# A third staging buffer, earlier loads of a group's mixes, and down products woven between them, in a one-core hybrid encoder layer

## The chip, the core and the metric

The kernel runs on one core of a Trainium2 chip. The core has five engines, each with a queue of its own that it works through in order: TensorE (PE; its weight loads are listed apart as PEld), VectorE (DVE), ScalarE (ACT), GpSimd (POOL) and SyncE (SP), which here issues nearly all of the DMAs. An instruction that has to wait holds up everything behind it in its engine's queue. The metric is the time in microseconds (us) from start to end of one execution.

## The reference, cut to what matters

One encoder layer over 2048 prompt rows and 128 sample rows (8 sequences of 16), 17 tiles of 128 rows:

```
h = _rms(x, ln1_g)
p = h @ w_in
q, k, v, p_rw = jnp.split(p, (ATT_Q, ATT_Q + ATT_KV, ATT_COLS), axis=-1)
...
rw, wkv, shift_last = _rwkv(p_rw, shift_prev, wkv0, ...)
x = x + jnp.concatenate([att, rw], axis=-1) @ w_out
u = jax.nn.relu(_rms(x, ln2_g) @ w_up)
x = x + (u * u) @ w_down
```

`att` is attention over a window of 192 keys with a learned sink, 8 query heads on 2 key heads. `_rwkv` is a recurrence that runs from one tile to the next (a state of 64 x 64 for each of 8 heads), which the kernel does in chunks of 64 rows, with a small triangular solve for each chunk. D_MODEL is 1024, the hidden width 4096.

## The kernel before, in words

Every large product is done as three fp32r products (high part times high part, high times low, low times high), so a weight is held as a pair `w2` of a high and a low half, 1024 columns each. The first time that a weight is used, its raw fp32 copy is loaded into a staging tile `ws`; ACT casts the high half (line 128), POOL subtracts to get the low half (two instructions, line 131), and POOL's queue stores the pair to DRAM as `wp` (line 133). Every later use loads the pair straight from `wp` (line 120).

The work has two phases. In the first, four groups of tiles are projected (`project`, line 204, PE). In the second, `feed_forward`, five groups go through the output projection (`out_proj`, L1175), the norm, `up` (L1217, 32 weights) and `down` (L1239, 16 pairs of weights, each one product of 512 columns for a tile and a half of the output). The groups are tiles 0-2, 3-5, 6-8, 9-11, and 12-15 with the sample tile. The first of them (group 0) uses every weight for the first time.

The side streams run beside these main loops: attention (`att_stream`, one tile after another), the preparation of a tile's recurrence (`prep_stream`, `rw_prep` and `solve`) and the recurrence itself (`chain_stream`). `Weaver` is a planner that writes out the program's order: each yield of the main loop adds its assumed cost to a clock, and a side stream is stepped when its due time has come. A stream's step says how many units its result will need (`r[0]`) and what it costs (`r[1]`); its next step is due at `clock + r[0] * pace`. One pace holds for all streams: 0.75 in the first phase, 0.88 in the second. A scheduler then sorts each engine's queue further, from a model of when each instruction could start. So all orders are fixed when the program is built.

Between the phases `wv.finish(att)` steps the streams until attention has ended; only then are the pools of the second phase opened. At the start of a group its tiles' *mixes* (the rows of attention and recurrence side by side, `mr`, in DRAM) are loaded into `ws` (`load_mix`, L1102), split into a high and a low part (`ghh`, `ghl`; ACT L83 and DVE L84), and the half that is not yet transposed goes through PE (L1130). `ws` is one pool of two buffers, shared by the mixes and the raw weights. `Group.stages` gives four steps, one mix each and a flush that emits the last transposes; a step emits the transposes of the mix before it. After these four steps follow the six products of the old group's last `down`, and then the new group's output projection.

Of the kernel before, what the change touches and what calls it, by code (L numbers as in the profile page):

```python
# [1 line left out]

# [5 lines left out]
F32 = mybir.dt.float32  # L8
# [6 lines left out]
P = 128  # L15
D = 1024
# [17 lines left out]
def hymba_kernel(  # L34
# [52 lines left out]
    def pool(stack, name, **kw):  # L87
        kw.setdefault("reuse_waits", "tile")
        return stack.enter_context(tc.tile_pool(name=name, bufs=1, **kw))
# [27 lines left out]
    def weight_parts(key, w2, n, stage, src):  # L117

        if key in parts:
            sy.dma_start(out=w2.bitcast(F32), in_=parts[key])  # L120
            return
        ws = stage()
        if callable(src):
            src(ws)
        else:
            sy.dma_start(out=ws, in_=src)
        wh, wl = w2[:, 0:n], w2[:, n:2 * n]
        ac.copy(out=wh, in_=ws)  # L128
        for c0 in range(0, n, 512):
            c = slice(c0, min(c0 + 512, n))  # L130
            gp.tensor_tensor(out=wl[:, c], in0=ws[:, c], in1=wh[:, c].bitcast(F32), op=ALU.subtract)  # L131
        parts[key] = dram.tile([P, 2 * n], F32, name=f"wp{len(parts)}")
        gp.dma_start(out=parts[key], in_=w2.bitcast(F32))
# [768 lines left out]

    class Weaver:
        def __init__(self):
            self.clock, self.mains, self.pace = 0.0, [], 0.75

        def add(self, gen):
            m = [gen, self.clock, None]
            self.mains.append(m)
            return m  # L910

        def step(self):

            for m in self.mains:
                if m[1] > self.clock or (m[2] and not m[2]()):
                    continue
                m[2] = None
                try:
                    r = next(m[0])
                except StopIteration:  # L920
                    self.mains.remove(m)
                    return True
                if callable(r):
                    m[2] = r
                else:
                    self.clock += r[1]
                    m[1] = self.clock + r[0] * self.pace
                return True
            return False

# [80 lines left out]
    def att_stream(atp):  # L1011
        for t in range(NTP):
            yield lambda: bool(roped)
            yield from att_tile(t, atp, roped.pop(0))


# [3 lines left out]
    def prep_stream():  # L1020
        for j, t in enumerate(order):
            yield lambda: (t, 8) in projected
            if j and order[j - 1] == SMP:
                yield lambda: SMP in done
            loaded = rw_load(t)
            yield 6, 0
            g = rw_prep(t, rp, loaded, rwc["so"][j % 2])
            for r in g:
                if r != "tail":
                    yield r  # L1030
                    continue
                yield lambda: j == 0 or order[j - 1] in done
                try:
                    next(g)
                except StopIteration as e:
                    ready.append(e.value)
            yield 1, 1

    def chain_stream():
        for t in order:  # L1040
            yield lambda: bool(ready)
            pr = ready.pop(0)
            yield 3, 0
            yield from rw_sample(pr, rp) if t == SMP else rw_chain(pr, rp, STB)
            done.add(t)

    wv = Weaver()
# [7 lines left out]
    with ExitStack() as sst:  # L1055
        m = wv.add(att_sample(pool(sst, "satt")))
        wv.run(in_proj(first, (3, 4, 5)))
        wv.finish(m)
    ast = ExitStack()
    atp = pool(ast, "att")  # L1060
    att = wv.add(att_stream(atp))
    wv.add(rope_stream(atp))
    wv.run(in_proj(first, (6, 7, 8), group_of(1)))
    rw_constants()
    chain, prep = wv.add(chain_stream()), wv.add(prep_stream())
# [8 lines left out]
    cp = pool(ctx, "cp")  # L1074
# [4 lines left out]
    def load_w(key, src):  # L1079

        w2 = cp.tile([P, 2048], F32R, name="w2", bufs=3)
        weight_parts(key, w2, 1024, lambda: cp.tile([P, 1024], F32, name="ws", bufs=2), src)
        return w2[:, 0:1024], w2[:, 1024:2048]

    def load_wout(n):
# [12 lines left out]
    loaded = {}  # L1098

    def load_mix(t):  # L1100
        m = cp.tile([P, D], F32, name="ws", bufs=2)
        sy.dma_start(out=m, in_=mr[t])  # L1102
        return m

# [144 lines left out]
    members = [[0, 1, 2], [3, 4, 5], [6, 7, 8], [9, 10, 11], [12, 13, 14, 15, SMP]]  # L1249
# [13 lines left out]
    def steps(todo):  # L1263
        for c, fn in todo:
            g = fn()
            if c:
                yield c
            elif g:
                yield from g

    def feed_forward():
        def wait_for(tiles):
            while not done.issuperset(tiles):
                yield None

        def loads(g):
            return [(0, lambda t=t: g.load_y(t)) for t in g.tiles]

        yield from wait_for(members[0])
        cur, last = group(0), None  # L1280
        mixes, rest = cur.stages()
        yield from steps(loads(cur) + mixes + rest)
        for g in range(LAST + 1):
            todo, nxt = [], None
            for i in range(32):
                if i == 31 and 0 < g < LAST - 1 and done.issuperset(members[g + 1]):
                    for t in members[g + 1][0:2]:
                        loaded[t] = load_mix(t)
                yield from cur.up(i)
                if i == 0 and last:  # L1290
                    yield from last
                if g == LAST - 1 and nxt is None and len(done) == len(order):
                    nxt = group(g + 1)
                    mixes, rest = nxt.stages()
                    todo = loads(nxt) + mixes + rest
                if i >= 2 and i % 2 == 0:
                    yield from cur.down(i // 2 - 1)
                if todo:
                    k = -(-len(todo) // (32 - i))
                    yield from steps(todo[:k])  # L1300
                    todo = todo[k:]
            last = cur.down(15)
            if g < LAST and nxt is None:
                if g == LAST - 1:
                    yield from last
                    last = None
                yield from wait_for(members[g + 1])
                nxt = group(g + 1)
                mixes, rest = nxt.stages()
                yield from steps(mixes)  # L1310
                if last:
                    yield from last
                    last = None
                yield from steps(loads(nxt) + rest)
            cur = nxt
        yield from last

    wv.pace = 0.88
    wv.run(feed_forward())


# [103 lines left out]
```

## Time and profile before

| | us |
|---|---|
| median of 3 runs | 3117.43 |
| lowest and highest | 3111.29 and 3127.98 |
| the profiled execution, its own time | 3127.03 |
| its span, first to last instruction | 3125.2 |
| PE busy in the span | 2924.8 (94%) |
| DVE busy | 1797.7 (58%) |
| ACT busy | 910.8 (29%) |
| POOL busy | 737.3 (24%) |

The profiled execution is one of its own and lies 0.3% above the median of the three. PE is busy nearly all the time, so the table alone doesn't show where time could be lost. For that one reads stretches: how long PE was busy in each, and at which clock ("PEclk" is the share of full speed that was granted, 1.00 or 0.50 at any moment, and a mean in between over a stretch). In a row of waits, "PE x <- DMA y" says that PE's next instruction x started only when the DMA into y had landed.

### The profile page before, as it was taken

What the parts mean: (1) busy time and instruction counts of PE and PEld (TensorE: products, weight loads), DVE (VectorE), ACT (ScalarE), POOL (GpSimd) and SP (SyncE); (2) the same over time, 40 slices, a digit from 0 to 9 for tenths busy, and PEclk for the clock granted to TensorE, in tenths of its full rate; (3) what the DMA queues carried; (4) which work ended last, traced back from release to release, by engine and by line L of the source; (5) the groups of instructions that cost most, each with busy time, mean ns of one, the idle gap of its engine ahead of it and who ended that gap; (6) DMA issues with size and microseconds to landing.
All of it is one profiled execution on the core that took longest, in us unless ns stands there. A gap on an engine that the chain in (4) does not pass through costs nothing. (4 is left out here: it accounts for less than half of the span.)

```text
span 3125.2 us, 52326 instructions
## 1 busy us (share of the span) xinstructions
PE 2924.8 (94%) x20566; PEld 2569.7 (82%) x20566; DVE 1797.7 (58%) x3386; ACT 910.8 (29%) x2398; POOL 737.3 (24%) x713
## 2 busy tenths in 40 slices
PE   7888999998997989989999989999999999999999
PEld 7776877887886878778888878888888899999988
DVE  3346677564577586785666764666764424433444
ACT  5234335234333434332222223122232102111111
POOL 4553232231434566661110110111010000000000
PEclk8888998999998999999999998999999999999999
DMA  7665563664655778886666664666655756544443
GB/s 255 217 227 171 175 195 113 199 201 135 215 194 184 255 294 305 296 297 238 211 233 206 230 246 163 239 223 205 236 209 206 287 199 223 188 149 150 154 154 142
DMA packets 195089, 657.67 MB, mean 210 GB/s; under 512 B 33302, under 2 KB 92454, under 8 KB 148763
## 3 DMA queue, kind: packets, MB, share of 16 engines
q1 hardware_dynamic: 179290, 557.58, 53.0%
q0 software_dynamic: 15552, 96.74, 7.6%
q8 instruction: 163, 2.67, 0.3%
q14 instruction: 84, 0.68, 0.1%
HBM read 486.32 MB, written 154.68 MB: 205 GB/s over the span
## 5 line engine op out<-in xcount | busy, mean ns | idle before, releaser
L1217 PE MATMUL ffn<-ghh,w 128*128 128x384 f32 (+1 forms) x3072 | 779.7, 330 | 1.1 <-DVE ghl L138 0.6
L1239 PE MATMUL ffn<-w,sh 128*128 128x512 f32 x2176 | 706.8, 406 | 28.6 <-ACT sh L1223 13.0
L1217 PEld LDWEIGHTS ffn<-ghh,w 128*128 128x128 f32 x3072 | 546.6, 189 | 10.9 <-issue 4.1
L1241 DVE SCALAR_TENSOR_TENSOR y<-ffn,rs,y 128x512 f32<-128x512 f32 x544 | 401.1, 747 | 199.2 <-PE ffn L1239 197.6
L1239 PEld LDWEIGHTS ffn<-w,sh 128*128 128x128 f32 x2176 | 408.8, 193 | 122.2 <-ACT sh L1223 16.0
L1217 PE MATMUL ffn<-ghl,w 128*128 128x384 f32 (+1 forms) x1536 | 504.9, 329 | 0.0
L204 PE MATMUL acc<-w,hh 128*128 128x304 f32 (+1 forms) x2128 | 466.8, 311 | 37.5 <-DMA w<-wp 17.8
L1239 PE MATMUL ffn<-w,sl 128*128 128x512 f32 x1088 | 431.6, 401 | 1.7 <-DVE sl L1224 1.7
L204 PEld LDWEIGHTS acc<-w,hh 128*128 128x128 f32 x2128 | 355.0, 196 | 62.7 <-issue 19.9
L204 PE MATMUL acc<-w,hl 128*128 128x304 f32 (+1 forms) x1064 | 321.9, 305 | 0.3 <-DVE hl L138 0.3
L1222 DVE TENSOR_TENSOR tq<-tq 128x384 f32<-128x384 f32 (+1 forms) x192 | 113.6, 592 | 348.7 <-ACT tq L1221 347.8
L1217 PEld LDWEIGHTS ffn<-ghl,w 128*128 128x128 f32 x1536 | 290.2, 189 | 6.4 <-issue 1.9
L1221 ACT ACTIVATE tq<-ffn 128x384 f32<-128x384 f32 (+1 forms) x192 | 91.0, 474 | 687.8 <-PE ffn L1217 642.9
L1239 PEld LDWEIGHTS ffn<-w,sl 128*128 128x128 f32 x1088 | 209.1, 192 | 50.3 <-DVE sl L1224 3.3
L131 POOL TENSOR_TENSOR w<-ws,w 128x512 fp32r<-128x512 f32 (+1 forms) x166 | 216.6, 1324 | 133.4 <-ACT w L128 129.3
L204 PEld LDWEIGHTS acc<-w,hl 128*128 128x128 f32 x1064 | 208.8, 197 | 3.9 <-issue 3.0
L1223 ACT CAST sh<-tq 128x384 fp32r<-128x384 f32 (+1 forms) x192 | 95.1, 495 | 367.2 <-PE ffn L1239 204.2
L228 POOL TENSOR_TENSOR ev<-ev,eb 128x304 f32<-128x304 f32 x102 | 101.8, 1001 | 249.8 <-DVE eb L220 155.5
L1224 DVE TENSOR_TENSOR sl<-tq,sh 128x384 fp32r<-128x384 f32 (+1 forms) x192 | 118.9, 620 | 67.9 <-ACT sh L1223 67.2
L1175 PE MATMUL ffn<-w,ghh 128*128 128x256 f32 x768 | 152.2, 298 | 5.5 <-ACT w L128 2.8
L1175 PEld LDWEIGHTS ffn<-w,ghh 128*128 128x128 f32 x768 | 125.9, 200 | 10.6 <-ACT w L128 3.2
L209 ACT ACTIVATE ev<-acc,xr_rs 128x304 f32<-128x304 f32 (+1 forms) x153 | 76.0, 502 | 192.0 <-PE acc L204 111.1
(335 smaller groups left out, 4239.7 us busy)
## 6 DMA issues: line engine op xcount, KB each, us to landing
w<-wp SPq DMA_DIRECT2D x288, 1024.0 KB
wp<-w POOLq DMA_DIRECT2D x72, 1024.0 KB, 7.5
w<-wp SPq DMA_DIRECT2D x72, 608.0 KB
w<-wp SPq DMA_DIRECT2D x36, 512.0 KB
ws<-in_wup_dram SPq DMA_DIRECT2D x32, 512.0 KB
ws<-in_wdn_dram SPq DMA_DIRECT2D x32, 512.0 KB
pa<-ev SPq DMA_DIRECT2D x102, 152.0 KB
xs<-pa SPq DMA_DIRECT2D x68, 228.0 KB
```

The costliest lines, as they stand in the source:

```text
L131: gp.tensor_tensor(out=wl[:, c], in0=ws[:, c], in1=wh[:, c].bitcast(F32), op=ALU.subtract)
L204: pe.matmul(acc[:, 0:n], a[:, kk], b[:, c], start=(kk == 0 and m == 0), stop=(kk == 7 and m == 2))
L209: ac.activation(out=ev, in_=acc[:, 0:n], func=AF.Copy, scale=hT[t][2])
L228: gp.tensor_tensor(out=ev, in0=ev, in1=eb, op=ALU.subtract)
L1175: pe.matmul(pss[j // 2][:, o:o + 256], a[:, kk, self.col(t)], w[:, c], start=(kk == 0 and m == 0 and j % 2 == 0), stop=(kk == 7 and m == 2 ...
L1217: pe.matmul(ps, w[:, wc], a[:, kk, c], start=(kk == 0 and m == 0), stop=(kk == 7 and m == 2))
L1221: ac.activation(out=tq, in_=ps, func=AF.Relu)
L1222: ve.tensor_tensor(out=tq, in0=tq, in1=tq, op=ALU.mult)
L1223: ac.copy(out=sh[:, c], in_=tq)
L1224: ve.tensor_tensor(out=sl[:, c], in0=tq, in1=sh[:, c].bitcast(F32), op=ALU.subtract)
L1239: pe.matmul(ps, a[:, tc_], w[:, fc], start=(f == 0 and m == 0), stop=(f == 1 and m == 2))
L1241: ve.scalar_tensor_tensor(out=yt[:, c], in0=ps, scalar=self.rs2[t], in1=yt[:, c], op0=ALU.mult, op1=ALU.add)
```

## The change

Four things change.

1. The staging tiles `ws` get a third buffer, for mixes and raw weights alike.
2. While the last `up` of groups 1 and 2 is emitted, all three mixes of the next group are emitted as loads, not only the first two. (For the first group the loads stand in its own mix steps; for the last group in its own as well.)
3. The six products of the old group's last `down` no longer follow the mix steps in one block: after the second, the third and the fourth mix step two of them are emitted.
4. The pace is kept for each stream: attention's own stays 0.75 and becomes 0.5 from tile 12 on; the two recurrence streams have 0.75 in the first phase and 0.88 in the second, as before.

```diff
-            self.clock, self.mains, self.pace = 0.0, [], 0.75
-
-        def add(self, gen):
-            m = [gen, self.clock, None]
+            self.clock, self.mains = 0.0, []
+
+        def add(self, gen, pace=0.75):
+
+            m = [gen, self.clock, None, pace]
...
-                    m[1] = self.clock + r[0] * self.pace
+                    m[1] = self.clock + r[0] * m[3]
...
             yield lambda: bool(roped)
+            if t == 12:
+                att[3] = 0.5
             yield from att_tile(t, atp, roped.pop(0))
...
-        weight_parts(key, w2, 1024, lambda: cp.tile([P, 1024], F32, name="ws", bufs=2), src)
+        weight_parts(key, w2, 1024, lambda: cp.tile([P, 1024], F32, name="ws", bufs=3), src)
...
-        m = cp.tile([P, D], F32, name="ws", bufs=2)
+        m = cp.tile([P, D], F32, name="ws", bufs=3)
...
-                    for t in members[g + 1][0:2]:
+                    for t in members[g + 1]:
                         loaded[t] = load_mix(t)
...
-                yield from steps(mixes)
+                for k, step in enumerate(mixes):
+                    yield from steps([step])
+                    for c in islice(last or (), 0 if k < 1 else 2):
+                        yield c
...
-    wv.pace = 0.88
+    chain[3] = prep[3] = 0.88
```

The instructions are the same ones, in the same number on every engine; only their order and the buffers change. Line numbers of the changed kernel are higher by one up to line 900 or so and by four from line 1079 to 1306 (L1102 becomes L1106, L1130 becomes L1134, L1239 becomes L1243).

SP's queue at the start of group 0, before: `ws` from `mr` is a mix, `ws` from `in_wout` a raw weight, `y` the rows of x, `bk` and `mr15` belong to the recurrence and to attention's last tile.

```order
L1102 DMA ws_10744<-mr0_108 128x1024
L1102 DMA ws_10755<-mr1_109 128x1024
L635 DMA bk1_11821<-kk_10777 64x512
L636 DMA bk1_11821<-E2_10771 64x512
L343 DMA mr15_123<-qk_10278 128x512
L1138 DMA y_10738<-in_x_prompt_dram 128x1024
L1138 DMA y_10740<-in_x_prompt_dram 128x1024
L1138 DMA y_10742<-in_x_prompt_dram 128x1024
L1102 DMA ws_10792<-mr2_110 128x1024
L1090 DMA ws_10806<-in_wout_dram 64x2x256 x4
L816 DMA mr3_111<-yw_10525 128x512
```

The same place in the changed kernel:

```order
L1106 DMA ws_10722<-mr0_108 128x1024
L1106 DMA ws_10733<-mr1_109 128x1024
L1106 DMA ws_10766<-mr2_110 128x1024
L637 DMA bk0_11828<-E2_10814 64x512
L637 DMA bk1_11829<-E2_10814 64x512
L344 DMA mr15_123<-qk_10102 128x512
L1142 DMA y_10716<-in_x_prompt_dram 128x1024
L1142 DMA y_10718<-in_x_prompt_dram 128x1024
L1142 DMA y_10720<-in_x_prompt_dram 128x1024
L1094 DMA ws_10780<-in_wout_dram 64x2x256 x4
L127 DMA ws_10881<-in_wout_dram 128x1024
L1094 DMA ws_10945<-in_wout_dram 64x2x256 x4
```

The third mix now stands right behind the first two, and three raw weights, not one, stand ahead of the recurrence's `mr3`.

DVE's queue at the same moment, before: L84 subtracts for the mixes (from `ws` directly, and from the transposed half `ffn`), L653, L666 and L668 are the solve of one tile, L811 to L815 the end of another tile's recurrence.

```order
L618 TENSOR_TENSOR m_11131<-rk,cst 128x4x64
L653 STREAM_TRANSPOSE WS<-ma 32x512 x4
L811 TENSOR_TENSOR yw<-yw,gn_rs 128x512
L659 MEMSET WS 128x16
L84 TENSOR_TENSOR ghl<-ws,ghh 128x4x128
L84 TENSOR_TENSOR ghl<-ffn,ghh 128x4x128
L666 TENSOR_TENSOR tm<-WS 128x8
L84 TENSOR_TENSOR ghl<-ws,ghh 128x4x128
L84 TENSOR_TENSOR ghl<-ffn,ghh 128x4x128
L668 TENSOR_REDUCE WS<-tm 128x2x2
```

And in the changed kernel:

```order
L619 TENSOR_TENSOR m_11143<-rk,cst 128x4x64
L812 TENSOR_TENSOR yw<-yw,gn_rs 128x512
L85 TENSOR_TENSOR ghl<-ws,ghh 128x4x128 x3
L815 TENSOR_TENSOR yw<-yw,bv 128x512
L619 TENSOR_TENSOR ma<-rk,cst 128x4x64
L619 TENSOR_TENSOR m_11143<-rk,cst 128x4x64
L85 TENSOR_TENSOR ghl<-ffn,ghh 128x4x128 x3
L816 TENSOR_TENSOR yw<-yw,gs 128x512
L654 STREAM_TRANSPOSE WS<-ma 32x512 x4
L660 MEMSET WS 128x16
```

All six subtractions of the mixes moved ahead of the solve's four transposes; before, the first four stood behind them and the last two later still. PE's queue follows suit: from the first product of the output projection to the first product of that solve (`sv`, L704) stand 60 rows of L1175 before and 110 after.

PE's queue at the start of group 3 (tiles 9-11), before: `ffn<-cst,ws` transposes a mix, L704 belongs to a solve, L1239 is the old group's last `down`.

```order
L1217 MATMUL ffn<-ghh,w_22607 128x384
L1130 MATMUL ffn<-cst,ws 128x128 x8
L704 MATMUL sv<-so_2899,t_22536 64x64 x16
L704 MATMUL sv<-tm,t_22536 64x64 x16
L1130 MATMUL ffn<-cst,ws 128x128 x4
L1239 MATMUL ffn<-w_22691,sh 128x512 x2
```

The same place in the changed kernel, up to the second L704:

```order
L1221 MATMUL ffn<-ghh,w_22609 128x384
L1134 MATMUL ffn<-cst,ws 128x128 x4
L1243 MATMUL ffn<-w_22675,sh 128x512 x2
L1243 MATMUL ffn<-w_22675,sl 128x512
L1243 MATMUL ffn<-w_22675,sh 128x512 x2
L1243 MATMUL ffn<-w_22675,sl 128x512
L705 MATMUL sv<-so_2899,t_22536 64x64 x16
L1134 MATMUL ffn<-cst,ws 128x128 x4
L1243 MATMUL ffn<-w_22675,sh 128x512 x6
L1243 MATMUL ffn<-w_22675,sl 128x512
L1243 MATMUL ffn<-w_22675,sh 128x512 x2
L1243 MATMUL ffn<-w_22675,sl 128x512 x3
```

Six down products now stand between the first transposes and the solve, and twelve between the solve's first sixteen matmuls and its next (which follow the last row here); the third mix's transposes come eighteen products after the first's. The starts of groups 1 and 2 read alike.

## Rows read from the trace of the kernel before

**Rows 1.** The page: TensorE's busy time, share and instructions.

```profile
PE 2924.8 (94%) x20566; PEld 2569.7 (82%) x20566; DVE 1797.7 (58%) x3386; ACT 910.8 (29%) x2398; POOL 737.3 (24%) x713
```

**Rows 2.** Busy time of each engine by stretch; then granted clock, DMA share, GB/s.

```profile
944.00:970.00 26.00, 21.20 (x204) 16.61 (x204) 18.62 (x45) 15.79 (x56) 3.41 (x3) 0.87 0.28 77
970.00:1001.00 31.00, 15.28 (x105) 13.58 (x103) 30.10 (x49) 7.03 (x11) 17.11 (x14) 0.67 0.76 260
1051.00:1412.00 361.00, 335.20 (x2192) 284.73 (x2193) 267.84 (x395) 133.92 (x262) 230.42 (x206) 0.96 0.79 285
1412.00:1431.00 19.00, 13.03 (x114) 9.83 (x113) 10.56 (x17) 6.11 (x10) 6.14 (x6) 0.66 0.59 211
1826.00:1837.00 11.00, 7.08 (x35) 5.73 (x34) 5.44 (x10) 7.67 (x25) 1.64 (x1) 0.72 0.55 192
2244.00:2255.00 11.00, 7.42 (x58) 6.03 (x53) 7.51 (x16) 6.47 (x18) 0.73 (x1) 0.69 0.61 227
2436.00:2446.00 10.00, 6.48 (x24) 4.90 (x23) 4.43 (x7) 1.79 (x3) 0.00 (x0) 0.83 1.02 419
```

**Rows 3.** Waits: us in total, times, longest (PE: whole run; ACT: 985 to 1410).

```profile
PE ffn L1130 <- DMA ws<-mr: 14.8, 4, 8.4
...
PE ffn L1239 <- ACT w L128: 3.9, 2, 2.6
...
ACT w L128 <- DMA ws<-in_wup_dram: 45.6, 19, 5.0
```

**Rows 4.** Timeline of PE, start of group 0; idle time before in brackets.

```profile
979.73 1.11 PE L1130 MATMUL ffn<-cst,ws 128*128 128x128 f32 x4 [8.37 <-DMA ws<-mr]
983.63 0.80 PE L1175 MATMUL ffn<-w,ghh 128*128 128x256 f32 x2 [2.79 <-ACT w L128]
...
1000.04 1.02 PE L704 MATMUL sv<-so,ma 64*64 64x64 f32 x26 [1.94 <-DVE so L689]
```

**Rows 5.** Timeline of SP's queue, start of group 0.

```profile
960.96 0.91 SPq L1102 DMA_DIRECT2D ws<-mr  x2
...
975.75 0.33 SPq L1102 DMA_DIRECT2D ws<-mr  x1
977.49 2.67 SPq L1090 DMA_DIRECT2D ws<-in_wout_dram  x4
```

**Rows 6.** Timelines of DVE and of POOL, start of group 0.

```profile
970.15 4.20 DVE L653 STREAM_TRANSPOSE WS<-ma 32x512 f32<-32x512 f32 x4
...
975.01 0.67 DVE L84 TENSOR_TENSOR ghl<-ws,ghh 128x512 fp32r<-128x512 f32 x1
...
984.23 1.77 DVE L84 TENSOR_TENSOR ghl<-ws,ghh 128x512 fp32r<-128x512 f32 x1
...
983.66 3.48 POOL L131 TENSOR_TENSOR w<-ws,w 128x512 fp32r<-128x512 f32 x2 [1.99 <-ACT w L128]
...
990.58 2.56 POOL L131 TENSOR_TENSOR w<-ws,w 128x512 fp32r<-128x512 f32 x2 [2.51 <-ACT w L128]
```

**Rows 7.** Timeline of PE at the starts of groups 1, 2 and 3.

```profile
1415.04 1.15 PE L704 MATMUL sv<-so,ma 64*64 64x64 f32 x32 [2.29 <-DVE so L689]
1419.84 1.11 PE L1130 MATMUL ffn<-cst,ws 128*128 128x128 f32 x4 [3.66 <-DMA ws<-mr]
...
1830.10 1.29 PE L594 MATMUL rk<-cst,E 128*128 128x128 f32 x8 [2.48 <-ACT art L595]
1832.82 1.12 PE L1130 MATMUL ffn<-cst,ws 128*128 128x128 f32 x4 [1.44 <-DMA ws<-mr]
...
2246.43 1.25 PE L704 MATMUL sv<-tm,t 64*64 64x64 f32 x32 [2.25 <-ACT tm L717]
2249.01 1.11 PE L1130 MATMUL ffn<-cst,ws 128*128 128x128 f32 x4 [1.33 <-DMA ws<-mr]
```

**Rows 8.** The chain that ended last: start, us, what; undisturbed runs of two products.

```profile
2261.34 2.87 PE ffn L1175 x24
...
2335.03 4.32 PE ffn L1239 x18
```

More of the change, by code (lines that the diff above doesn't have):

```diff
@@ L1 @@
 from contextlib import ExitStack
+from itertools import islice
 import concourse.bass as bass
```

## The prediction

> **What bounds the kernel now.** The page comes first: TensorE is busy for 94% of the span and no other engine for more than 58% [rows 1]. So the kernel ends when PE's queue ends, and time can only come from two places: gaps in that queue, and stretches in which PE runs at the lower of its two clocks (1.2 instead of 2.4 GHz, a granted clock of 0.50 in the rows). The second view is the busy time by stretch [rows 2]. Its length minus PE's busy time is the gap; busy time times one minus the granted clock is roughly what the lower clock cost. The reader should see that the losses sit at the places that the change touches: the start of group 0 (970 to 1001) has 15.7 us of gaps in 31 us, at a mean clock of 0.67; the starts of groups 1, 2 and 3 (1412, 1826, 2244) have 6.0, 3.9 and 3.6 us of gaps, and clocks of 0.66, 0.72 and 0.69. Group 0's body (1051 to 1412) loses 25.8 us in gaps, spread thin. The third view, the waits, names who ends the gaps: PE's transposes of a mix waited four times for the load of that mix, 14.8 us in all, and PE waited twice for the cast of a raw weight, 3.9 us [rows 3]. Timelines then show each place.
>
> **The change, part by part.** Every engine executes the same instructions, so nothing is added or removed as work; each term is a wait that goes or comes.
>
> *Start of group 0.* SP issues the loads of mixes 0 and 1 at 960.96, but that of mix 2 only at 975.75, and the first raw weight at 977.49 [rows 5]: both had to wait until DVE had read a staging buffer. DVE's reading (L84, 0.67 us each) stood behind 4.20 us of solve transposes, from 970.15, and began at 975.01 [rows 6]. PE idled 8.37 us for mix 2 and 2.79 us for the first weight, and reached the solve's first product at 1000.04, after 1.94 us more of waiting for DVE [rows 4]. In the changed order mix 2 is loaded with the others, the six L84 come ahead of the 4.20 us, so three buffers come free early and three raw weights follow at once. But DVE was busy for 30.10 of the 31 us [rows 2], and its work only changes order, so the solve will not be ready much before 1000. What is gained is what PE has done by then: 110 rows of L1175 instead of 60. One such product takes 0.12 us (2.87 us for 24 [rows 8]), so 50 of them are 6 us. **Term: -6.** Bounds: 0, if the solve is late by as much as PE is early, and -10, about two thirds of the 15.7 us of gaps.
>
> One rule speaks against this term. The row shows an L84 of 1.77 us, against 0.67 us undisturbed, beside a pair of POOL subtractions of 3.48 us, against 2.56 us [rows 6]: two engines that slowed each other. The Trainium skill, page "SBUF — State Buffer", section "SBUF: two separate sides", says that VectorE with two SBUF inputs and GpSimd share a port pair as an exclusive lock, so one waits for the other. The rows agree, with 1.1 and 0.9 us for one meeting. The L84 now come before any POOL subtraction, but these come forward into the solve's own two-input work; if three of them met it, the term would be -3 instead of -6 and the sum -22 instead of -25. I keep -6, since POOL's work keeps its amount.
>
> *Starts of groups 1 to 3.* The gaps are six waits: three for a mix's load, 3.66, 1.44 and 1.33 us, and three for the recurrence, 2.29, 2.48 and 2.25 us [rows 7]; they sum to 13.4 us, as the stretches' gaps do. The lower clock adds 13.03 x 0.34 + 7.08 x 0.28 + 7.42 x 0.31 = 8.7 us [rows 2]. Every third mix now has a buffer of its own, and at groups 2 and 3 its load stands far earlier in SP's queue; at group 1 it is covered by the down products instead. So the 6.4 us of mix waits go. The recurrence's waits get cover: six down products between the first transposes and the solve, twelve and four transposes between the two solve steps at group 3. A down product takes 0.24 us (4.32 us for 18 [rows 8]), so that is 1.4 us and 3.4 us, against waits of 2.3 to 2.5 us; I take 5 of the 7.0 us. Of the lower clock I take 5 of 8.7 us, since PE's gaps mostly vanish. **Term: -16.** Bounds: -6, the mix waits alone, and -22, everything. What covered the splitting of the new mixes were the same down products; now the third mix has only six of them behind it (1.4 us), but the output projection begins with the half that needs no transposing, so I charge nothing for that; without this cover it would be one ACT and one DVE step, about 1.3 us by the L84 row, three times.
>
> *Raw weights in group 0.* ACT waited 45.6 us for raw up weights, 19 times [rows 3]. SP could load one only when POOL had read an old one. Most of this is hidden, since PE has products to do meanwhile; what reached PE is the 3.9 us of waits for the cast [rows 3]. **Term: -4**, bounds 0 and -6 (with a share of lower clock as at the groups' starts, 8.7 on 13.4).
>
> *Last group.* Between 2436 and 2446 PE lost 3.5 us of gaps and 6.48 x 0.17 = 1.1 us of clock [rows 2]. But the DMA engines were full there (share 1.02, 419 GB/s [rows 2]): a third buffer moves one mix ahead and moves no fewer bytes. **Term: -1**, bounds 0 and -5.
>
> *Attention's last tiles.* From 944 to 970 PE has only side streams to do: gaps of 4.8 us, 2.8 us of clock [rows 2]. In the new order 116 rows, not 150, stand between the last projection and the first mix. **Term: -2**, bounds -6 and, if attention's DVE steps now delay the recurrence's, +4.
>
> *Given back.* PE's stalls gave DVE time to catch up; without them DVE is late next, at the casts and solves in group 0, where it is busy for 268 of 361 us [rows 2]. **Term: +4**, bounds 0 and +12, half of the 25.8 us of gaps there.
>
> The sum is -6 - 16 - 4 - 1 - 2 + 4 = -25 us. The profiled execution took 3127.0 us, so it would take 3102; it lies 9.6 us above the median of the three runs shown, 3117.4, and on that footing the forecast is 3092 us. All bounds at their best give -49 (3068), all at their worst +10 (3127).
>
> **The rivals.** *A: the waits change their name.* PE's gaps at the groups' starts go, but come back as waits for DVE a few us later, since the recurrence has the same work to do per tile. For it: three of the six waits of [rows 7] are the recurrence's, and DVE was full at the start of group 0. Against it: in the body of group 0 DVE had 93 of 361 us free. Then only the mix waits of groups 1 to 3 are kept, with a little of the start: -8, 3109 us.
>
> *B: it does not do what it says.* The loads are earlier in SP's queue, but the DMA engines deliver them no earlier. For it: a DMA share of 0.76 to 1.02 in [rows 2]. Against it: the mix of 975.75 waited for a buffer, not for the engines. -3, 3114 us.
>
> *C: slower, through ACT's queue.* With raw weights there earlier, the cast L128 waits no longer for its input but for a free pair `w2` (three buffers, as before), which PE frees. In ACT's queue the cast then holds up the relu and cast behind it (L1221, L1223), on which PE's next products wait. The price is that of one cast wait, up to 2.6 us [rows 3]. Group 0 has 64 such weights; from the tenth such wait on (25 / 2.6) the gain is gone, and one weight in four makes 16 x 2.6 = 42 us: 3134 us. For it: those 19 waits of ACT must find a next reason. Against it: ahead of each L1221 ACT's queue holds as many L128 in both kernels, give or take one.
>
> **How the numbers follow.** Chances: the forecast 0.64, A 0.20, B 0.09, C 0.07. About 0.5% (15.6 us) is what a measurement of this kernel can tell from no change. Nearly all of the forecast's range (3068 to 3101) is faster by more than that, A and B are within it, C is slower: faster 0.63, same 0.30, slower 0.07. The range from 3068 to 3119 takes in the forecast, A and B; it leaves out C and the far ends.
>
> **What would show it.** In the profile after: no PE wait for `ws` from `mr` longer than a microsecond at groups 0 to 3; three mix loads side by side on SP near 960 and the first L1175 some 4 us after the mixes, with the first L704 still about 30 us after 970; clocks above 0.9 at the starts of groups 1 to 3; ACT's waits for raw weights well below 45.6 us with no waits of L128 for PE in their place. Wrong it would be if PE's waits for DVE and ACT results (L704, L1239) grew by more than 10 us in sum, if gaps remain where they were at the groups' starts, or if the end of attention came later than 970.

## The result, and the profile after

The changed kernel takes 3078.93 us (median of 4 runs, 3074.63 to 3083.32) against 3117.40 us of before in the same series: a ratio of 0.9874, 95% interval 0.9850 to 0.9898. That is 38.5 us less, where 25 were forecast. The profiled execution took 3074.63 us (span 3072.8), the one of before 3127.03. Of the 52.4 us between these two, 13.9 are scatter: the one of before lay 9.6 us above its median, that of after 4.3 us below.

The page, TensorE's line: busy share and count as in [rows 1], with less busy time because more of it runs at the full clock (granted clock 0.965 in the mean of the span, 0.957 before).

```profile
PE 2896.5 (94%) x20566; PEld 2554.5 (83%) x20566; DVE 1807.6 (59%) x3386; ACT 908.8 (30%) x2398; POOL 736.4 (24%) x713
```

Busy time by stretch, columns as in [rows 2]: attention's tail after the last projection, the start of group 0 up to its first `up`, and the starts of groups 1, 2 and 3.

```profile
937.00:959.90 22.90, 19.26 (x199) 14.64 (x198) 19.76 (x40) 16.23 (x51) 10.26 (x7) 0.93 0.49 144
959.90:1033.80 73.90, 55.38 (x484) 51.07 (x483) 46.01 (x88) 24.66 (x48) 38.41 (x37) 0.84 0.84 283
...
1391.00:1411.50 20.50, 16.96 (x103) 12.26 (x101) 19.18 (x30) 6.08 (x11) 5.51 (x5) 0.83 0.77 266
1800.50:1814.50 14.00, 13.46 (x86) 11.01 (x85) 10.99 (x19) 8.50 (x28) 4.13 (x3) 1.00 0.69 252
2198.00:2212.00 14.00, 14.00 (x136) 11.29 (x135) 11.76 (x22) 8.46 (x22) 1.29 (x1) 1.00 0.72 257
```

The starts of groups 2 and 3 have hardly a gap (0.54 us and none) and nothing of the lower clock any more. Group 1's start still has 3.5 us of gaps, and there DVE was busy for 19.18 of 20.5 us.

PE's waits over the whole run (total, times, longest). The four waits for a mix at groups 0 to 3 [rows 3] are gone. New are two waits at group 0's output projection, 7.6 and 6.9 us.

```profile
PE ffn L1179 <- DVE y L1184: 8.3, 2, 6.9
...
PE ffn L1179 <- DVE tm L667: 7.6, 1, 7.6
PE ffn L1243 <- DVE y L1245: 6.9, 8, 2.4
PE ffn L1243 <- ACT sh L1227: 5.7, 6, 2.5
...
PE sv L705 <- DVE so L690: 4.3, 3, 2.3
```

The timeline of PE at the start of group 0, which answers to [rows 4]: the transposes of all three mixes run at once, and then PE waits 7.57 us, and later 6.93 us for one of DVE's additions. The solve's first product (L705) follows at 996.63.

```profile
959.89 1.53 PE L1134 MATMUL ffn<-cst,ws 128*128 128x128 f32 x12
...
971.35 0.80 PE L1179 MATMUL ffn<-w,ghh 128*128 128x256 f32 x2 [7.57 <-DVE tm L667]
...
990.09 0.80 PE L1179 MATMUL ffn<-w,ghh 128*128 128x256 f32 x2 [6.93 <-DVE y L1184]
...
996.63 0.33 PE L705 MATMUL sv<-so,ma 64*64 64x64 f32 x2 [0.54 <-DVE so L690]
```

SP's queue at the same place, which answers to [rows 5]: three mix loads side by side, but the first raw weight only at 962.11, when the first mix had left its staging buffer.

```profile
949.94 1.39 SPq L1106 DMA_DIRECT2D ws<-mr  x3
...
962.11 2.66 SPq L1094 DMA_DIRECT2D ws<-in_wout_dram  x4
```

ACT cast that weight at 970.25, and PE began when the cast ended:

```profile
970.25 1.04 ACT L129 CAST w<-ws 128x1024 fp32r<-128x1024 f32 x1 [2.73 <-DMA ws<-in_wout_dram]
```

So the wait put down to DVE's `tm` is one for the first weight; the kernel e7 below, with the same order there, has 6.9 us at this place under the name of the cast.

ACT's waits from 972 to 1390. The 45.6 us for raw `up` weights [rows 3] are gone, and the cast (L129) now waits for a pair `w2` that PE frees.

```profile
ACT w L129 <- PE ffn L1179: 27.1, 5, 10.6
...
ACT w L129 <- PE ffn L1243: 8.9, 10, 2.7
```

### The profile page after: what moved, and what is told of

Its sections match the earlier page's. It is cut to its first block, busy times and chain, and to the rows that moved or that the text cites. A ratio compares the mean times of both kernels' runs of the same rounds, so it can differ in the third digit from the quotient of the medians.

```text
span 3072.8 us, 52320 instructions
## 1 busy us (share of the span) xinstructions
PE 2896.5 (94%) x20566; PEld 2554.5 (83%) x20566; DVE 1807.6 (59%) x3386; ACT 908.8 (30%) x2398; POOL 736.4 (24%) x713
## 5 line engine op out<-in xcount | busy, mean ns | idle before, releaser
L1243 PE MATMUL ffn<-w,sh 128*128 128x512 f32 x2176 | 695.4, 402 | 21.0 <-DVE y L1245 6.9
L205 PE MATMUL acc<-w,hh 128*128 128x304 f32 (+1 forms) x2128 | 466.0, 311 | 34.9 <-DMA w<-wp 13.9
L1243 PEld LDWEIGHTS ffn<-w,sh 128*128 128x128 f32 x2176 | 403.8, 190 | 111.9 <-DVE y L1245 10.3
L1243 PE MATMUL ffn<-w,sl 128*128 128x512 f32 x1088 | 426.8, 397 | 1.9 <-DVE sl L1228 1.9
L1226 DVE TENSOR_TENSOR tq<-tq 128x384 f32<-128x384 f32 (+1 forms) x192 | 121.1, 631 | 342.6 <-ACT tq L1225 341.6
L1243 PEld LDWEIGHTS ffn<-w,sl 128*128 128x128 f32 x1088 | 206.3, 190 | 49.8 <-DVE sl L1228 3.9
L1228 DVE TENSOR_TENSOR sl<-tq,sh 128x384 fp32r<-128x384 f32 (+1 forms) x192 | 112.1, 584 | 62.7 <-ACT sh L1227 61.7
```

What stands on the lines that cost most here:

```text
L205: pe.matmul(acc[:, 0:n], a[:, kk], b[:, c], start=(kk == 0 and m == 0), stop=(kk == 7 and m == 2))
L1226: ve.tensor_tensor(out=tq, in0=tq, in1=tq, op=ALU.mult)
L1228: ve.tensor_tensor(out=sl[:, c], in0=tq, in1=sh[:, c].bitcast(F32), op=ALU.subtract)
L1243: pe.matmul(ps, a[:, tc_], w[:, fc], start=(f == 0 and m == 0), stop=(f == 1 and m == 2))
```

## The experiments

Eleven kernels were run. They are compared in stretches that begin at the last projection (the last row of L204), for a reason that the last section gives. **Tail** is from there to the first mix transposes; **start 0** from these to group 0's first `up`; **body 0** from there to its last `up`; **starts 1-3** the sum of the three stretches from a group's last `up` to the next group's first output projection product; **A** is from the last projection to the first product of group 1's output projection, **B** from there to the last group's. What follows B is 627 us in every kernel. All in us, one profiled execution each; the ratio is to the kernel before in the same series, whose median lies between 3113.7 and 3117.8 us.

| kernel | median | ratio (95%) | tail | start 0 | body 0 | starts 1-3 | A | B |
|---|---|---|---|---|---|---|---|---|
| before | 3117.4 | 1 | 30.8 | 80.8 | 360.4 | 65.1 | 497.6 | 1060.8 |
| after | 3078.9 | 0.9874 (0.9850-0.9898) | 22.9 | 73.9 | 357.2 | 47.6 | 474.4 | 1034.2 |
| e1 buffer | 3091.8 | 0.9923 (0.9908-0.9938) | 30.5 | 72.2 | 352.5 | 51.4 | 478.5 | 1037.5 |
| e2 weave | 3103.3 | 0.9957 (0.9942-0.9972) | 30.8 | 79.4 | 359.1 | 58.2 | 500.4 | 1030.6 |
| e3 pace | 3105.2 | 0.9965 (0.9947-0.9982) | 22.0 | 83.5 | 353.5 | 63.0 | 484.1 | 1051.8 |
| e4 no weave | 3085.4 | 0.9904 (0.9885-0.9922) | 22.6 | 74.9 | 350.8 | 51.7 | 471.9 | 1035.7 |
| e5 no pace | 3089.3 | 0.9926 (0.9907-0.9946) | 30.5 | 74.6 | 353.9 | 48.0 | 479.9 | 1036.9 |
| e6 third mix | 3091.7 | 0.9933 (0.9911-0.9954) | 22.4 | 78.1 | 362.3 | 50.5 | 486.1 | 1042.5 |
| e7 two early | 3080.1 | 0.9879 (0.9856-0.9903) | 22.4 | 73.6 | 357.6 | 47.6 | 473.9 | 1036.2 |
| e8 first weight | 3079.8 | 0.9896 (0.9871-0.9920) | 22.5 | 73.5 | 353.5 | 52.3 | 474.6 | 1034.9 |
| e10 pace 0.3 | 3082.4 | 0.9903 (0.9888-0.9918) | 27.0 | 67.6 | 355.0 | 48.2 | 470.7 | 1037.9 |
| e11 early group 1 | 3075.7 | 0.9875 (0.9853-0.9896) | 23.6 | 74.6 | 352.9 | 53.6 | 477.4 | 1030.7 |
| e12 POOL subtracts | 3074.3 | 0.9867 (0.9843-0.9891) | 22.4 | 80.7 | 345.8 | 47.8 | 469.6 | 1036.6 |

The stretches don't hold the same work in every kernel. Counted where each begins, start 0 has 517 matmuls before, 483 in after and 455 to 561 elsewhere, because steps of the recurrence move between it and body 0. So start 0 alone doesn't show what an edit is worth. Start 0 and body 0 together have 2698 to 2705 matmuls in every kernel and can be compared: 441.2, 438.5, 436.9 and 440.4 us where raw weights have two buffers (before, e2, e3, e6), and 422.6 to 431.2 us in the nine kernels where they have three. (The profiled executions of before, e2 and e6 lie 5 to 10 us above their medians, that of e3 2 us below.) Busy time of before in these two stretches, then of e6; the count of matmuls here takes in those that overlap an edge:

```profile
970.30:1051.10 80.80, 60.46 (x518) 54.16 (x516) 49.19 (x100) 29.47 (x61) 44.88 (x40) 0.79 0.78 272
1051.10:1411.50 360.40, 334.70 (x2188) 284.27 (x2189) 267.30 (x393) 133.84 (x261) 230.32 (x206) 0.96 0.79 286
```

```profile
965.50:1043.50 78.00, 58.10 (x528) 53.30 (x528) 48.23 (x103) 28.64 (x60) 42.53 (x40) 0.85 0.80 281
1043.50:1405.80 362.30, 338.96 (x2172) 287.23 (x2171) 271.49 (x383) 134.13 (x260) 229.40 (x206) 0.96 0.78 284
```

**e1: the third buffer alone,** on the kernel before.

```diff
-        ... name="ws", bufs=2)
+        ... name="ws", bufs=3)
```

> The third buffer alone, on the kernel before. Theory (each gain belongs to the part that the prediction gave it to): start of group 0 -6, raw weights -4, last group -1, and at the starts of groups 1 to 3 the waits for mixes, 6.4 us, with their share of the lower clock (8.7 us on 13.4 of gaps), so -10: together -21, about 3096 us; the recurrence's waits stay at the groups' starts. Rival 1 (the waits change their name: without the weaving, the transposes that no longer wait for a mix stand behind the recurrence's waits, which grow by as much): only start, raw weights and last group are left, -11, about 3106 us. Rival 2 (what was gained is an accident of the order, not of the buffer): any time, with group 0's transposes still waiting.

26.1 us faster in its series (3117.84 to 3091.77). The theory's size holds, rival 1 falls: the starts of groups 1 to 3 lose 13.7 us without any weaving. Start 0 is 8.6 us shorter, but by work that left it (62 matmuls, 10.2 us of PE's busy time) and not by its gaps, which are 22.0 us instead of 20.3. What the theory did not say is where the start of group 0 loses time now. In the timeline of PE the wait for mix 2 is gone, and one for the first weight stands in its place:

```profile
992.60 0.79 PE L1175 MATMUL ffn<-w,ghh 128*128 128x256 f32 x2 [11.18 <-ACT w L128]
```

**e2: the weaving alone,** on the kernel before.

```diff
-                yield from steps(mixes)
+                for k, step in enumerate(mixes):
+                    yield from steps([step])
+                    for c in islice(last or (), 0 if k < 1 else 2):
+                        yield c
```

> The weaving alone, on the kernel before: two buffers, two mixes loaded early. Theory: six or twelve down products cover the third mix's load as well as the recurrence's waits, so most of the 13.4 us of gaps at the starts of groups 1 to 3 goes, with its clock: -16, about 3101 us, while the start of group 0 keeps its 8.4 us wait for mix 2 and its 2.8 us wait for the first weight. Rival 1 (the third buffer is what takes the mix waits away, and the third mix's load still waits for a buffer): only the recurrence's part, about -8, 3109 us. Rival 2 (the waits change their name): -3 or less, 3114 us.

14.5 us faster: the theory's size, but not its place. Starts 1 to 3 give 6.9 us in all, while B is 30.2 us shorter; 10.2 us of that lie in group 2's output projection and norm (64.1 us to 53.9). At groups 2 and 3 weaving by itself empties the starts as well as the buffer does (13.2 and 14.0 us, of 20.2 and 19.3). At group 1 it makes the start longer, 31.0 us instead of 25.6, with 32 more matmuls of the solve in it. SP's queue shows one reason: with two buffers, the third of that group's mixes is loaded only behind a raw weight of the last `down`, and the next raw weight (1430.22) behind that mix:

```profile
1422.53 0.33 SPq L127 DMA_DIRECT2D ws<-in_wdn_dram  x1
1429.79 0.32 SPq L1103 DMA_DIRECT2D ws<-mr  x1
1430.22 0.37 SPq L127 DMA_DIRECT2D ws<-in_wdn_dram  x1
```

PE then waits for that weight's cast, with the third mix's transposes behind it:

```profile
1438.65 0.80 PE L1240 MATMUL ffn<-w,sh 128*128 128x512 f32 x1 [3.91 <-ACT w L129]
```

**e3: the pace alone,** on the kernel before, with a pace for each stream as in the change.

```diff
...
+            if t == 12:
+                att[3] = 0.5
...
```

> Attention's pace alone, on the kernel before. Theory: it shortens the end of attention, -2 as predicted or -7 as the trace of the changed kernel reads (from attention's 898 row to its last store 71.8 us before, 64.7 after), and nothing behind it: 3110 to 3115 us, with first transposes some 7 us earlier and group 2's output projection as long as before (64 us). Rival (the pace shifts the recurrence against the groups, so that other waits go, the 9 us of group 2's output projection among them): -15 or more, 3102 us or below.

12.6 us faster, more than the theory, less than the rival. The tail is 8.8 us shorter, and body 0 6.9 us; start 0 gives 2.6 us back: 12 more matmuls stand in it, and PE still waits for mix 2 there, 9.01 us. Group 2's output projection and norm took 59.0 us, neither the 64.1 of before nor the 54.7 of after.

**e4: the change without the weaving.**

> The changed kernel without the weaving: the old group's six last down products stand in one block behind the mix steps again. Theory: mixes have their buffer and are loaded early, so only the cover of the recurrence's waits is lost, 5 to 7 us of gaps with their clock: +8, about 3087 us, with the starts of groups 1 to 3 each some 3 us longer. Rival 1 (the weaving is what empties the starts, and the early loads do nothing by themselves): +17, about 3096 us. Rival 2 (the weaving does nothing that the buffer does not): the changed kernel's 3079 us.

3085.35 us: the theory (+8; by the medians 6.4 came, by the ratios 9.4). Starts 1 to 3 are 4.1 us longer, 3.3 of them at group 1; rival 1 falls. Rival 2 is told apart by these starts alone, since the intervals of the two ratios overlap. Once there is a third buffer, weaving pays at group 1 and little elsewhere: B is 1.5 us longer.

**e5: the change without the pace.**

> The changed kernel with attention's pace left at 0.75 throughout; buffer, early loads and weaving stay. Theory (the pace shortens the stretch from the last projection to the first mix transposes, 30.8 us in the three kernels without it and 22 to 22.9 us in the three with it, and does nothing behind it): that stretch is 31 us again and the time +8, about 3087 us. Rival 1 (most of what the pace alone brought, 12.6 us, came from later stages, through a shifted recurrence): +12 or more, 3091 us or above, with longer stretches at groups 1 and 2. Rival 2 (the next work is late anyway, so the shorter tail is given back at the start of group 0): +2 or less, 3081 us.

3089.25 us, and the tail is 30.5 us again. The place is the theory's, the size lies between it and rival 1 (+10 by the medians, +16 by the ratios, +8.2 by the traces from the last projection on). How the pace pays is in the busy time by stretch. The first phase up to the last projection, tail and start 0 of e5:

```profile
0.00:940.40 940.40, 836.26 (x6401) 728.66 (x6402) 530.56 (x1130) 368.39 (x1089) 344.36 (x376) 0.93 0.58 191
940.40:970.90 30.50, 25.70 (x262) 19.54 (x261) 22.83 (x50) 17.70 (x60) 6.84 (x7) 0.89 0.33 100
970.90:1045.50 74.60, 51.16 (x456) 48.69 (x455) 46.13 (x89) 25.07 (x48) 42.53 (x38) 0.82 0.85 286
```

The first phase of after:

```profile
0.00:937.00 937.00, 834.18 (x6451) 727.46 (x6452) 538.16 (x1140) 369.15 (x1098) 339.77 (x376) 0.94 0.59 192
```

With the pace 62 matmuls of attention and the recurrence leave the tail (258 to 196), and 50 more run before the last projection (6401 to 6451). In e3 the same 62 leave and the same 50 come. So most of the work that left the tail moved forward, into the first phase. What it costs there can't be told: the first phase ends anywhere from 937.0 to 950.1 us in these kernels. Start 0 has 28 matmuls more than in e5 (455 to 483, 51.16 to 55.38 us of busy time) at nearly the same length, 74.6 and 73.9 us: its gaps take them up (23.4 us in e5, 18.5 in after).

**e6: the third buffer for a third mix only;** raw weights stay at two.

```diff
-        ... lambda: cp.tile([P, 1024], F32, name="ws", bufs=3), src)
+        ... lambda: cp.tile([P, 1024], F32, name="ws", bufs=2), src)
...
-        m = cp.tile([P, D], F32, name="ws", bufs=3)
+        own = t < 12 and t % 3 == 2
+        m = cp.tile([P, D], F32, name="mx" if own else "ws", bufs=1 if own else 2)
```

> The changed kernel with the third buffer given to mixes alone: the third mix of groups 0 to 3 has a staging tile of its own, and raw weights rotate through two buffers as before. Theory (raw weights are worth the predicted 4 us and more: without the third buffer for them group 0's body is some 7 us longer, by the 360.4 us of before against 352.5 with the buffer alone): ACT's waits for raw up weights are back at some 45 us, and the time is +4 to +8, 3083 to 3087 us. Rival (those waits of ACT are hidden behind PE's own work, and the third buffer pays by the mixes alone): the waits come back but the time stays at 3079 us.

3091.68 us, +12.8 by the medians and +18 by the ratios (0.0059 of 3117): beyond the theory's 8, and the rival falls. ACT's waits for raw weights are back, as its waits from 960 to 1430 show:

```profile
ACT w L129 <- DMA ws<-in_wup_dram: 39.3, 14, 5.7
ACT w L129 <- DMA ws<-in_wdn_dram: 33.4, 15, 5.9
...
ACT w L129 <- DMA ws<-in_wout_dram: 28.3, 4, 14.3
```

A is 486.1 us, no shorter than e3's 484.1, which has two buffers for everything, and start 0 and body 0 together, 440.4 us, are as long as without any third buffer: up to group 1 the third buffer pays by the raw weights, not by the mixes. By which waits of PE it pays isn't shown; those for the relu's cast (L1223 before) are 13.0 us before and 5.7 in after, but 13.1 in e1. The mixes' buffer shows at starts 1 to 3, which are 12.4 us shorter than e3's and 7.7 shorter than e2's, which has the weaving.

**e7: only two mixes loaded early.**

```diff
-                    for t in members[g + 1]:
+                    for t in members[g + 1][0:2]:
```

> The changed kernel with only two of a group's three mixes loaded early, as before; the third is loaded in its own mix step. DVE's, ACT's and POOL's queues are the same as the changed kernel's; on SP the third load stands a few rows later, at groups 2 and 3 alone. Theory (buffer and weaving empty these starts, not the earlier load): the starts of groups 2 and 3 stay at 13.6 us each and the time at 3079 us, within 3. Rival (the third load's place on SP is what takes away the waits of 1.4 and 1.3 us for it): +3 to +5, 3083 us, with those two waits back.

3080.06 us, starts of 13.7 and 13.5 us, no wait for a mix at groups 2 and 3: the theory. The earlier third load does nothing that shows beside the buffer and the weaving.

**e8: the first raw weight loaded ahead.**

```diff
...
+        first = cur.pl.tile([P, D], F32, name="y", bufs=cur.nt)
+        load_wout(0)(first)
+        ahead["out", 0, 0] = first
```

> The changed kernel, with the first raw weight of group 0's output projection loaded ahead of the mixes, into a tile that one row of x takes over later. Theory (at the start of group 0 PE now waits 7.6 us for this weight, whose load stands on SP until a mix has left its staging buffer; the same place where the kernel with the buffer alone waited 11.2 us for the cast): that wait goes to below 1 us, the first product of the output projection comes some 7 us earlier, and since the second weight can't come earlier by as much, 4 us of it remain, one weight's products (36 of 0.12 us): 3075 us. Rival 1 (DVE is what paces this start, and its solve is no earlier): PE waits as long a little later, 3079 us. Rival 2: the second weight comes as much earlier too, and 7 us remain, 3072 us.

3079.82 us: rival 1's time, but not its mechanism. The first product comes 6.2 us after the first transposes instead of 11.5 (a wait of 2.35 us is left for the cast, then 2.27 for POOL's half), but from there to the first `up` it takes 67.3 us instead of 62.5, so that start 0 is 73.5 us, as in after. It holds 46 matmuls more, though (483 to 529), and its gaps are 13.1 us instead of 18.5: what filled the time is moved work, not a later wait. Start 0 and body 0 are 427.0 us (431.1 in after), but group 1's start is 25.1 instead of 20.4, and A is the same. The load itself moved only from 2.2 us after the first transposes to 0.7 us before them.

**e10: pace 0.3.** The 0.5 of the change becomes 0.3.

> The changed kernel with attention's pace 0.3 instead of 0.5 from tile 12 on. Theory (attention's end is bound by its own chain from step to step once its steps are emitted early enough; 0.5 has most of it): from the last projection to the first mix transposes 20 to 23 us, time within 3 us of 3079. Rival 1 (steps emitted earlier still go on paying as from 0.75 to 0.5): another -5, 3074 us. Rival 2 (attention's steps then delay the recurrence on DVE, which group 0 needs later): +4 or more, 3083 us.

3082.40 us: the time is the theory's; its tail is not (27.0 us, at a granted clock of 0.72), and start 0 is shorter by as much and more (67.6). The two together are 94.6 us against 96.8 of after. They hold 44 matmuls fewer; 28 more run before the last projection and 35 more in body 0, so work changed its stretch again.

**e11: two mixes of group 1 loaded early.**

```diff
-                if i == 31 and 0 < g < LAST - 1 and ...
-                    for t in members[g + 1]:
+                if i == 31 and g < LAST - 1 and ...
+                    for t in members[g + 1][0:3 if g else 2]:
```

> The changed kernel, with the first two mixes of group 1 also loaded while the last up of the group before is emitted; in the changed kernel they wait on SP behind raw weights, and group 1's start is 20.4 us long where those of groups 2 and 3 are 13.6. Theory (late mixes make the difference): group 1's start some 4 to 7 us shorter, 3074 us. Rival 1 (the raw weights of the last up and down, which now come later on SP, are then what PE waits for): the start no shorter, 3079 to 3083 us. Rival 2 (the recurrence sets this start): no change.

3075.68 us, within the scatter of after. Group 1's start is 26.3 us, some 6 longer than in after, and not shorter (e8, without this edit, has 25.1): its busy time shows the same DVE work as after (19.53 to 19.18 us) in a longer stretch, and more gaps.

```profile
1397.00:1423.50 26.50, 19.22 (x97) 13.55 (x96) 19.53 (x30) 5.98 (x11) 6.56 (x6) 0.74 0.63 226
```

That is on the side of rival 1, though PE's waits there bear the names of casts, of mix subtractions and of the solve, none of a raw weight, so its mechanism isn't shown. What it lost there doesn't appear in the time, which can't be told from after's.

**e12: e8, and group 0's direct subtractions on POOL.**

```diff
-            evac_split(...)
+            ac.copy(out=self.hh[:, 0:4, c], in_=src)
+            en = gp if t < 3 else ve
+            en.tensor_tensor(out=self.hl[:, 0:4, c], in0=src, in1=..., op=ALU.subtract)
```

> The kernel with the first weight loaded ahead, and in group 0 the three subtractions on the untransposed halves of the mixes on POOL instead of DVE. Loading the first weight ahead took the wait of 7.6 us away and gave it back as waits for DVE's solve (10.4 us), so DVE seems to set when group 0's output projection ends. Theory: three subtractions, 3.0 us in a row in the trace, leave DVE's queue ahead of the solve, so the stretch from the last projection to group 0's first up is 2 to 3 us shorter than 96.0 us, 3076 us. Rival 1 (another engine or the second weight sets it by now): 96 us as before, 3080 us. Rival 2 (the subtractions on POOL hold back the recurrence's work there or slow DVE's): longer by 2 us or more, 3082 us.

3074.34 us, not to be told from after (the intervals overlap). Start 0 is 80.7 us, rival 2's side, while body 0 is 345.8 us, the shortest of all; A together is 469.6 us against 474.6 of e8. Start 0 has 561 matmuls here (529 in e8), and with body 0 it takes 426.5 us, as in e8 (427.0). Its expectation also misread e8: the three waits for the solve, 10.4 us, lie in body 0 and at group 1's start, not in start 0. Whether DVE alone bounds start 0 stays open.

## Why the prediction was right, and where not

**Starts of groups 1 to 3 (-16).** They went from 65.1 to 47.6 us: -17.5. The mechanism is the one given: mix waits to the buffer, the recurrence's to the cover. The split was not foreseen: the buffer alone brings 13.7 us, weaving alone 6.9, so the two largely mend the same gaps, and B is 1030.6 to 1037.5 us with either or both. Clocks above 0.9 came at groups 2 and 3 (1.00), not at group 1 (0.83).

**Start of group 0 (-6).** It went from 80.8 to 73.9 us: -6.9. The pivot of the working held: the solve's first product came at 996.63, 59.7 us after the last projection (60.5 before), with 110 rows of the output projection done instead of 60, and from there to the first `up` 37.2 us passed instead of 51.1. The way there was another. The first product came 9.9 us after the mixes' transposes had ended, not some 4, because the first weight needs a staging buffer too and three buffers hold three mixes. PE's waits for the first weights and for DVE's additions at that output projection grew from 3.9 us to 15.0 (7.6, 6.9 and 0.5), more than the 8.4 us of the mix wait that went. Start 0 got shorter mostly because it holds 34 matmuls of the recurrence fewer (5.1 us less of busy time); its gaps fell by 1.8 us only, from 20.3 to 18.5. Body 0 has 27 matmuls more and is 3.2 us shorter all the same, with gaps of 18.1 us instead of 25.7. Over both stretches the change brings 10.1 us, and e6, where the mixes have their buffer and these stretches still take 440.4 us, puts that on the raw weights.

**Raw weights (-4).** Mis-sized. The working counted the 3.9 us for which PE was seen to wait for a cast, and of ACT's waits those for `up` weights alone. From 985 to 1410 ACT waited longer still for the other raw weights (in after, from 972 to 1390, 8.3 and 1.7 us):

```profile
ACT w L128 <- DMA ws<-in_wout_dram: 34.8, 7, 7.5
ACT w L128 <- DMA ws<-in_wdn_dram: 30.9, 15, 4.6
```

Start 0 and body 0 take 439.3 us in the mean with two buffers for raw weights and 427.2 with three, 12 us less; by e6 the whole of it is 11.7 us in A and 12.8 us in the time (18 by the ratios), outside the bound of 6. This term and the one before together were forecast at -10 and measured at -10.1, but that the sum fits is luck: nearly all of it belongs to the raw weights.

**Attention's last tiles (-2).** The other mis-sized step, beyond its bound of -6 too. The four kernels without the pace have tails of 30.5 to 30.8 us, those with 0.5 have 22.0 to 23.6. The working counted gaps and lower clock in the tail (7.6 us, of which it took 2), though the order that it quoted (116 rows instead of 150) showed that work leaves the tail; where it goes was the question, and e5 answers it: 50 of the 62 matmuls run before the last projection.

**Last group (-1).** 178.1 to 174.5 us, with 173.8 to 178.2 in the other kernels: no more than their scatter.

**Given back (+4).** It took another place: PE's waits for DVE and ACT at `sv` and at `down` did not grow, they fell by some 11 us over the run (41 to 30 in sum). What was given back lies at the output projection inside start 0, 11.1 us of new waits. The parts alone bring, by ratio, 24, 13 and 11 us (0.0077, 0.0043 and 0.0035 of 3117), together 48, and the change 39; with intervals of 5 to 8 us on each of these, the times don't settle how much the parts overlap.

**A place without a term.** Group 2's output projection and norm went from 64.1 to 54.7 us, with gaps of 3.7 us instead of 8.9. They take 53.9 to 57.4 us in the nine kernels with the weaving and 59.0 to 59.8 in the three changed ones without it (e1, e3, e4), so part of it is the weaving's. How it comes about is open.

**Rivals.** A (waits change their name) holds at start 0 only, where PE now waits for the first weight (7.6 us) and for DVE's addition (6.9 us). B falls: the mixes come earlier. C's condition came true, ACT's casts now wait for a pair `w2` (27.1 and 8.9 us, above), but not its price: PE's waits for the relu's cast did not grow (13.0 us in 7 waits before, 5.7 after). Why the measured time lies 13 us below the forecast is thus, as far as one pair of profiles tells, the tail (5.9 us beyond its term), group 2's output projection and norm, and the 4 us that were not given back.

## To carry to other kernels

When a staging buffer is shared by two uses, count the waits of both and of the loads queued behind them: here, up to group 1, its third copy paid by the raw weights, whose waits on ACT looked hidden, and not by the mixes, whose wait was the longest. Edits that fill the same gap need not add up, so run each alone and leave each out. And before two stretches are compared, count the work in them: start 0 got shorter by work that moved out of it, and the tail by work that moved ahead of the last projection.

## What the hardware showed that was not expected

**The same order of instructions runs at different clocks.** e4 and after have the same PE queue until the last `up` of group 0, and yet body 0 took 350.8 and 357.2 us, at these granted clocks. Busy time of e4, and then of after:

```profile
1043.50:1394.30 350.80, 332.65 (x2216) 286.12 (x2217) 271.38 (x396) 135.83 (x272) 235.20 (x208) 0.97 0.81 295
```

```profile
1033.80:1391.00 357.20, 339.14 (x2217) 290.94 (x2216) 273.22 (x398) 137.09 (x273) 235.60 (x210) 0.95 0.79 290
```

The first phase scatters more: in before and e1 PE's queue is the same up to the first products of group 0's output projection, and the last row of the projection began at 939.5 and 949.5 us. This is why the stretches above begin there, and why a difference of some 6 us in one stretch of one profile is no finding.

**POOL's subtractions stretch DVE's small steps.** In the solve at the start of group 0, one and the same step of DVE took 1.02 us in after, beside four of POOL's subtractions, and 0.24 us in e1, where POOL was idle. DVE and POOL of after, then DVE of e1:

```profile
974.21 1.02 DVE L667 TENSOR_TENSOR tm<-WS 128x50 f32<-128x50 f32 x1
...
971.37 5.00 POOL L132 TENSOR_TENSOR w<-ws,w 128x512 fp32r<-128x512 f32 x4 [5.06 <-DMA ws<-in_wout_dram]
```

```profile
991.93 0.24 DVE L666 TENSOR_TENSOR tm<-WS 128x50 f32<-128x50 f32 x1
```

The Trainium skill, page "SBUF — State Buffer", section "SBUF: two separate sides", has the two engines share a port pair as an exclusive lock; these rows agree, and the subtractions did come forward into the solve as the prediction feared. What that cost PE is not shown; start 0 and body 0 together gained 10.1 us all the same.
